# Wider idle matrix products, an earlier second row tile and reordered norms in the first stage of a hybrid decoder block

## The chip, the cores and the metric

The kernel runs on one core of one Trainium2 chip. The metric is the device time in microseconds (us) of one execution; lower is better. The engines are TensorE (PE, with its weight loads as PEld), VectorE (DVE), ScalarE (ACT), GpSimd (POOL) and SyncE (SP, which issues the loads). TensorE works on 128 x 128 weights, and its clock can be halved by a gate; the profile shows the granted share.

## The reference, cut to what matters

One decoder layer on `x` of 1024 rows by 1024 columns in fp32. A conditioning vector gives a scale and shift per column (`mod`), with which the normed rows become `h`; then `h` is multiplied by a wide weight matrix, and two mixers and projections follow.

```python
mod = jax.nn.silu(c) @ ada_w + ada_b
shift, scale, gate = jnp.split(mod, 3, axis=-1)
h = rms_norm(x, norm_w) * (1 + scale[:, None, :]) + shift[:, None, :]
proj = h @ w_in
...
return x + gate[:, None, :] * (merged @ w_out)
```

Only the way from `x` and `c` to `h`, and the first columns of `h @ w_in`, are touched by the change.

## The kernel before

The first stage makes `h` transposed: columns of `x` on the partitions, rows on the free axis. It works in eight turns n = 0 to 7; turn n handles one tile of 128 columns, k = KS[n] with KS = (0, 4, 1, 5, 2, 6, 3, 7), and each turn has two halves h of 512 rows. `xt[t]` (t = 0 to 7) are the tiles of 128 rows of `x`, each 128 x 1024. In the profile a tile is named without its number: `x` for all of `xt`.

What happens to a row tile, in order: ACT squares it and sums (`square`; for t = 1 DVE does it, `square_v`), DVE adds epsilon and POOL raises to the power -0.5 (`factors`, result `rs`), and DVE multiplies the tile in place, 512 columns at a time (`normed(t, half, V)`; half 0 serves k < 4, half 1 the rest). `transposes(n, h)` then has PE transpose four 128 x 128 blocks into the PSUM tile `px`, and `rows_of_h(n, h)` applies scale and shift: it writes the fp32 result `hf`, its fp32r rounding (`b11h`, `b`, `b21h` and the like) and the rest that rounding left (`b11l` and so on).

What happens to the conditioning: three small loads land in `pk`; PE transposes it into `pp`; DVE copies it to `par` and makes silu(c) (`sc`, `scz`) with ACT's tanh. `matvec(n)` multiplies `scz` by a tile `aw` of the conditioning weights on PE into `pm`, ACT copies this out as `row`, `modulation_product(n)` turns it to the partitions on PE, and `modulation(n)` makes scale and shift `md` on DVE.

`first_products(n)` is a generator: each step issues one product of 512 columns of `h` by the first 256 columns of the weights, in fp32r, into the PSUM tiles `acc`. The weights `w0r` are split into `w0h` (ACT) and `w0l` (DVE) by `split_w0`. Turns 0 and 1 are written out by hand; from turn 2 on, `prepare(n)` returns the work that is placed between certain steps of the products.

The order on every engine is the order in which the code is written (the calls are pinned); each engine takes its instructions in that order and waits at each for what it needs. Loads go through SP's queue, in written order too.

`warm(n)` issues idle products: they multiply constants into the PSUM tile `pd`, whose contents are overwritten before use. They stand at five places, with 11, 4, 3, 10 and 5 of them: ahead of the transpose of `pk`, ahead of `matvec(0)`, ahead of `modulation_product(0)`, ahead of `transposes(0, 0)` and ahead of `transposes(0, 1)`. None stands between the transposes and the first `acc` product.

Of the kernel before, what the change touches and what calls it, by code (L numbers as in the profile page):

```python
# [16 lines left out]
P = 128  # L17
# [3 lines left out]
NCH = S // P  # L21
# [14 lines left out]
def hybrid_kernel(  # L36
# [7 lines left out]
    V, A, G, PE = nc.vector, nc.scalar, nc.gpsimd, nc.tensor  # L44
# [26 lines left out]
    def cst(shape, name, dt=F32):  # L71
        return const.tile(shape, dt, name=name, tag=name)
# [6 lines left out]
    pin = tc.keep_in_program_order  # L79

    def mm(acc, l, r, first=True, last=True):
        pin(PE.matmul(acc, l, r, start=first, stop=last))  # L82

    def tp(dst, src, idn):
        pin(PE.transpose(dst, src, idn))  # L85

    def f32(t):
        return t.bitcast(F32)

    def load(dst, src):  # L90
        pin(nc.sync.dma_start(dst, src))
# [4 lines left out]
    ident = cst([P, P], "ident")  # L96
    make_identity(nc, ident)
    ones = cst([P, P], "ones")
# [51 lines left out]
    def ax(name, tag="pm"):  # L150
        return psum0.tile([P, 512], F32, name=name, tag=tag, bufs=2 if tag == "px" else 1)
# [17 lines left out]
    def wide(name, dt=F32):  # L169
        return w4[0].tile([P, S], dt, name=name, tag="w4", bufs=w4[1])  # L170


    with tc.tile_pool(name="p0", bufs=1, reuse_waits="tile") as p0:
        pxs = {(0, 0): ax("px0_0", "px")}
        pp = ax("pp")
        pd = ax("pd", "pd")
# [3 lines left out]
        aw, wk = {}, {}  # L180
# [7 lines left out]
        def hf_tile(k, h):  # L188
            if k not in hf2:
                hf2[k] = wide(f"hf{k}")  # L190
            return hf2[k][:, h * 512 : (h + 1) * 512]
# [30 lines left out]
        def split_w0(n):  # L222
            raw, hi, lo = wk[n]
            pin(A.copy(hi, raw))
            pin(V.tensor_sub(lo, raw, f32(hi)))
# [14 lines left out]
        def late_loads():  # L240
            load(wd, w_in[:, COL_DT : COL_DT + NH].rearrange("(k p) c -> p k c", p=P))

        def warm(n):

            for _ in range(n):
                mm(pd[:, 0:P], ident, ones)

        warm(11)
        tp(pp[:, 0:P], pk, ident)
        pin(V.tensor_copy(par, pp[:, 0:P]))  # L250
        pin(V.tensor_scalar_add(par[:, 24:32], par[:, 24:32], 1.0))
# [6 lines left out]
        def matvec(n):  # L258

            pms[n] = pm = ax(f"pm{n}")  # L260
            for i in range(KT):
                q = i % 4
                mm(pm[32 * q : 32 * q + 32, 0:256], scz[:, i, :], aw[n][:, i].rearrange("p j c -> p (j c)"),
                   i < 4, i >= 4)
            row = p0.tile([P, 256], F32, name=f"row{n}", tag="row", bufs=2)
            pin(A.copy(row, pm[:, 0:256]))
            mds[n] = row

        def modulation_product(n):

            pm, row = pms[n], mds[n]
            for j in range(2):
                mm(pm[:, 256 + j : 257 + j], row[:, j * P : (j + 1) * P], ones[:, 0:1])

        def modulation(n):

            k, pm = KS[n], pms[n]
            md = p0.tile([P, 2], F32, name=f"md{n}", tag="md", bufs=3)
            pin(V.tensor_add(md[:, 0:1], pm[:, 256:257], par[:, 16 + k : 17 + k]))
            pin(V.scalar_tensor_tensor(md[:, 1:2], pm[:, 257:258], par[:, 24 + k : 25 + k], par[:, 8 + k : 9 + k],  # L280
                                       op0=ALU.add, op1=ALU.mult))
            mds[n] = md

        def transposes(n, h):
            k = KS[n]
            px = pxs[n, h] if n + h == 0 else ax(f"px{n}_{h}", "px")
            for i in range(4):
                tp(px[:, i * P : (i + 1) * P], xt[4 * h + i][:, k * P : (k + 1) * P], ident)
            pxs[n, h] = px

        def rows_of_h(n, h, meanwhile=None):
            k, md, px = KS[n], mds[n], pxs[n, h]
            if k < 4 and h:
                b12 = wide(f"b12_{k}", F32R)
                hh, hl = b12[:, 0:512], b12[:, 512:1024]
            else:
                nm = ("b11" if k < 4 else ("b21", "b22")[h])
                hh, hl = bop[nm][0][k % 4], bop[nm][1][k % 4]
            if n + h:
                hfs[k, h] = hf_tile(k, h)  # L300
            hf = hfs[k, h]
            if n + h:
                for t in (hh, hf):
                    pin(A.activation(t, px, AF.Identity, scale=md[:, 1:2], bias=md[:, 0:1]))
            else:
                pin(V.tensor_scalar(hf, px, md[:, 1:2], md[:, 0:1], op0=ALU.mult, op1=ALU.add))
                pin(V.tensor_copy(hh, hf))
            if meanwhile:
                meanwhile()
            pin(V.tensor_sub(hl, hf, f32(hh)))  # L310
            hhs[n, h] = (hh, hl)
# [6 lines left out]
        def t_sum(k, i):  # L318

            b11, b12, b21, b22 = (hfs[k + 4 * (j // 2), j % 2] for j in range(4))  # L320
            a, b, c = ((b11, b12, b11), (b12, b22, b12), (b22, b22, b11), (b21, b21, b22))[i]
            pin(V.tensor_sub(a, b, c))

        def t_part(k, nm):

            t_split(nm, k, hfs[{"t1": (k, 0), "t3": (k, 1), "t2": (k + 4, 1), "t4": (k + 4, 0)}[nm]])
# [11 lines left out]
        def dt_products(k):  # L338

            for q, (kk, h) in enumerate(((k, 0), (k + 4, 0), (k, 1), (k + 4, 1))):  # L340
                mm(pd[32 * q : 32 * q + 32, :], wd[:, kk, :], hfs[kk, h], k == 0, k == 3)

        def halves(n):

            return (0, 1) if KS[n] < 4 or n == 1 else (1, 0)
# [5 lines left out]
        def square(t):  # L351
            pin(A.activation(junk, xt[t], AF.Square, accum_out=sq0[:, t : t + 1]))

        def factors(a, b):
            bs = slice(a, b)
            pin(V.tensor_scalar_add(sq0[:, bs], sq0[:, bs], D * EPS))
            pin(G.tensor_tensor(rs[:, bs], sq0[:, bs], nhalf[:, bs], op=ALU.pow))

        def normed(t, half, eng):
            part = xt[t][:, half * 512 : (half + 1) * 512]  # L360
            if eng is A:
                pin(A.mul(part, part, rs[:, t : t + 1]))
            else:
                pin(V.tensor_scalar_mul(part, part, rs[:, t : t + 1]))
# [4 lines left out]
            pin(V.scalar_tensor_tensor(junk2, xt[t], 1.0, xt[t], op0=ALU.mult, op1=ALU.mult,  # L369
                                       accum_out=sq0[:, t : t + 1]))  # L370

        warm(4)
        square(0)
        factors(0, 1)
        square_v(1)
        factors(1, 2)
        matvec(0)
        warm(3)
        modulation_product(0)
        normed(0, 0, V)  # L380
        modulation(0)
# [8 lines left out]
        pin(V.tensor_sub(wk[0][2], wk[0][0], f32(wk[0][1])))  # L390
        for t in range(4, NCH):
            square(t)
        warm(10)
        transposes(0, 0)
        rows_of_h(0, 0, lambda: (factors(4, 5), factors(5, 6)))
        load_aw(2)
        load_w0(2)
# [10 lines left out]
        normed(7, 0, V)  # L408
        for t in range(1, 4):
            normed(t, 1, V)  # L410
        warm(5)
        transposes(0, 1)
        rows_of_h(0, 1)
        transposes(1, 0)
        for t in (4, 5):
            normed(t, 1, V)
        matvec(1)
        split_w0(1)
        for _ in range(2):
            next(start)  # L420
        modulation_product(1)
        modulation(1)
        for t in (6, 7):
            normed(t, 1, V)
        rows_of_h(1, 0)
        for _ in start:
            pass

        def prepare(n):

            a, b = halves(n)
            k = (n - 2) // 2

            def second():
                modulation_product(n)
                transposes(n, b)
                if n % 2 == 0:
                    dt_products(k)
                modulation(n)
                if n % 2:  # L440
                    t_sum(k, 2)
                    t_sum(k, 3)
                rows_of_h(n, a)
                if n % 2 == 0:
                    t_sum(k, 0)
                rows_of_h(n, b)
                if n % 2:
                    t_part(k, "t3")
                    t_part(k, "t2")
                else:  # L450
                    t_sum(k, 1)

            if n == 2:
                return {
                    4: lambda: (transposes(1, 1), rows_of_h(1, 1), matvec(n)),
                    8: lambda: (transposes(n, a), second()),
                }
            return {2: lambda: (matvec(n), transposes(n, a)), 7: second}
# [12 lines left out]
        for n in range(1, KT):  # L471
            todo = prepare(n + 1) if n + 1 < KT else {}
            for at, _ in enumerate(first_products(n), 1):
                if at == 1 and n + 2 < KT:
                    load_aw(n + 2)
                    load_w0(n + 2)
                if at in todo:
                    todo[at]()
                if at == 2 and n < KT - 1:
                    split_w0(n + 1)  # L480
                between(n, at)
# [1067 lines left out]
    fill = proj_a()  # L1549
# [68 lines left out]
    def slot_tile(name, dt=F32):  # L1618
        tag = room.pop(0)
        t = hp.tile([P, 512], dt, name=name, tag=tag)  # L1620
        tags_of[name] = tag
        return t
# [218 lines left out]
    for u, (nm, k) in enumerate(units):  # L1841
# [28 lines left out]
        if k == KT - 1:  # L1870
            for j in range(4):
                with tc.high_priority():
                    if nm in ("p1", "p3", "p5"):
                        t = slot_tile(f"{nm}_{j}")
# [200 lines left out]
```

## Time and profile before

| what | value |
|---|---|
| median of 3 runs | 1360.52 us (1359.84 to 1361.66) |
| the profiled execution | 1360.42 us |
| its span (first to last instruction) | 1358.4 us |
| PE busy | 1345.4 us, 99% of the span |
| DVE, ACT, POOL busy | 1055.1, 800.6, 198.8 us |
| chain that ended last | PE 92%, DVE 3%, DMA 3% |

The span is shorter than the execution by 2.0 us, which lie around it. The rows of a timeline give start, length, engine, line of the code, operation, tiles (output, then inputs), shape and the number of records that were merged into the row; in brackets stands the idle time of the engine ahead of it and what ended it. Rows overlap a little, because a matrix product's end lies behind the start of the next one. The first stage ends near 65 us.

### The profile page before, as it was taken

Reading aid. Unit: us, or ns where it says so; the run is one execution under the profiler, and the core shown is the slowest. Engines: PE = TensorE matmul, PEld = TensorE weight load, DVE = VectorE, ACT = ScalarE, POOL = GpSimd, SP = SyncE. Lnnn points to the kernel's source line nnn. Section 1 sums busy time; section 2 is a strip of 40 time slices with the busy share of each in tenths; the row PEclk is TensorE's granted clock in tenths of the full one; section 3 lists DMA queues with packets and bytes.
Section 4 is the critical chain, followed back from the end, with each engine's and each line's share of the span. In section 5 each row is a group of like instructions: output and inputs, shape, how many; then the busy total and the mean of one; then the engine's idle time right before and its main releaser. Section 6 shows DMA issues by size and latency. Waiting matters only on the chain.

```text
span 1358.4 us, 20100 instructions
## 1 busy us (share of the span) xinstructions
PE 1345.4 (99%) x6897; PEld 1112.8 (82%) x6897; DVE 1055.1 (78%) x1732; ACT 800.6 (59%) x1446; POOL 198.8 (15%) x197
## 2 busy tenths in 40 slices
PE   8999999999999999999999999999999999999997
PEld 6688888888888888888888888888888888888886
DVE  5777786687777888688887788458888877959976
ACT  5854666666666665466576655486877743233543
POOL 2000000000000000000000000007798981000002
PEclk9999999999999999999999999999999999999999
DMA  9675434433345667778656866489889987878913
GB/s 301 178 247 155 127 110 124 124 118 116 108 125 155 194 196 229 238 227 246 199 194 188 248 203 185 157 290 315 302 297 318 297 260 277 323 265 316 380 43 124
DMA packets 249577, 288.64 MB, mean 212 GB/s; under 512 B 16860, under 2 KB 196484, under 8 KB 249476
## 3 DMA queue, kind: packets, MB, share of 16 engines
q1 hardware_dynamic: 174868, 203.80, 47.2%
q10 hardware_dynamic: 74544, 83.57, 18.0%
q8 instruction: 54, 0.88, 0.3%
q14 instruction: 47, 0.39, 0.1%
q0 software_dynamic: 64, 0.00, 0.0%
HBM read 199.82 MB, written 87.49 MB: 212 GB/s over the span
## 4 chain that ended last, share of the span: by engine, by line
PE 92%; DVE 3%; DMA 3%; issue 1%; ACT 0%; SPq 0%; POOL 0%; POOLq 0%; DVEq 0%; ACTq 0%
PE pma L82 7%; PE xcb L584 6%; PE xuz L584 6%; PE xz L584 6%; PE xx L584 6%; PE xg L584 6%; PE yuz L584 3%; PE yx L584 3%; PE ycb L584 3%; PE yz L584 3%; PE vx L989 3%; PE yg L584 3%; PE ox L1913 3%; PE yi L82 2%; PE sp L82 2%; PE oy L1913 2%
## 5 line engine op out<-in xcount | busy, mean ns | idle before, releaser
L1158 POOL TENSOR_SCALAR_AFFINE_SELECT dcy<-dcy 128x1024 f32<-128x1024 f32 x32 | 35.3, 1104 | 788.3 <-ACT ea L1154 785.9
L1166 ACT ACTIVATE dcy<-dcy,nacs 128x128 f32<-128x128 f32 x256 | 78.3, 389 | 2.6 <-POOL dcy L1158 2.0
L1182 DVE TENSOR_TENSOR dcy<-dcy,pc 128x1024 f32<-128x1024 f32 x32 | 39.0, 1219 | 8.0 <-PE pc L85 5.8
L1264 POOL TENSOR_TENSOR yz<-y,sl 128x512 f32<-128x512 f32 x32 | 44.7, 1397 | 2.5
L82 PE MATMUL pma<-yh,wah 128*128 128x512 f32 x128 | 43.2, 418 | 0.0
L82 PE MATMUL pma<-yh,wal 128*128 128x512 f32 x128 | 42.6, 413 | 0.0
L82 PE MATMUL pma<-yl,wah 128*128 128x512 f32 x128 | 40.2, 395 | 0.0
L1154 ACT ACTIVATE ea<-dcy 64x512 f32<-64x512 f32 x64 | 39.8, 622 | 0.4
L1059 ACT ACTIVATE ac<-ac 128x1024 f32<-128x1024 f32 x32 | 33.9, 1060 | 10.2 <-DVE ac L1057 10.1
L1189 ACT COPY bn<-pc 128x256 f32<-128x256 f32 x32 | 11.9, 372 | 47.0 <-DVE dcy L1182 46.8
L1263 POOL TENSOR_TENSOR y<-y,ym 128x512 f32<-128x512 f32 (+1 forms) x32 | 37.5, 1171 | 1.7 <-DVE ym L1261 1.7
L1057 DVE SCALAR_TENSOR_TENSOR ac<-c2x,cwt,ac 128x1023 f32<-128x1023 f32 (+2 forms) x24 | 30.7, 1279 | 8.6 <-ACT ac L1055 8.5
L1057 DVE SCALAR_TENSOR_TENSOR ac<-c2cb,cwt,ac 128x1023 f32<-128x1023 f32 (+2 forms) x24 | 30.7, 1279 | 8.1 <-ACT ac L1055 8.0
L1928 POOL TENSOR_TENSOR r<-r,fnw 128x512 f32<-128x512 f32 x4 | 6.1, 1528 | 205.7 <-ACT junk L1926 205.7
L82 PE MATMUL yi<-dcy,xd 128*64 128x128 f32 x512 | 35.0, 279 | 0.0
L1652 DVE SCALAR_TENSOR_TENSOR yn<-yn,par,rb 128x512 f32<-128x512 f32 x32 | 26.1, 823 | 10.8 <-DMA yn<-yb_d 10.8
L1261 DVE TENSOR_TENSOR ym<-yn,ea 128x512 f32<-128x512 f32 (+1 forms) x32 | 19.9, 622 | 18.5 <-PE yn L82 18.4
L82 PE MATMUL sp<-xe,bn 128*128 128x256 f32 x112 | 32.7, 409 | 0.0
L82 PEld LDWEIGHTS yn<-sl,st 128*128 128x128 f32 x224 | 29.7, 191 | 2.8 <-POOL st L1227 0.4
L82 PEld LDWEIGHTS yi<-dcy,xd 128*64 128x64 f32 x512 | 27.3, 136 | 5.7 <-issue 3.2
L1057 DVE SCALAR_TENSOR_TENSOR ac<-c1cb,cwt,ac 128x1023 f32<-128x1023 f32 (+2 forms) x24 | 30.7, 1278 | 1.3 <-ACT ac L1055 1.3
L1021 ACT ACTIVATE vm<-vm,vr 128x128 f32<-128x128 f32 x64 | 25.5, 482 | 9.7 <-DMA vm<-v_d 9.2
(2985 smaller groups left out, 4369.6 us busy)
## 6 DMA issues: line engine op xcount, KB each, us to landing
sl<-s_d SPq DMA_DIRECT2D x32, 768.0 KB
s_d<-ac ACTq DMA_DIRECT2D x32, 512.0 KB
wb_d<-wbb ACTq DMA_DIRECT2D x32, 512.0 KB
dcy<-acs_d SPq DMA_DIRECT2D x32, 512.0 KB
av<-in_w_in_dram SPq DMA_DIRECT2D x36, 256.0 KB
aw<-in_ada_w_dram SPq DMA_DIRECT2D x16, 512.0 KB
wbr<-in_w_proj_b_dram SPq DMA_DIRECT2D x32, 256.0 KB
yb_d<-yz ACTq DMA_DIRECT2D x32, 256.0 KB
```

The source lines that it names most:

```text
L82: pin(PE.matmul(acc, l, r, start=first, stop=last))
L584: pin(PE.matmul(ps, lw[:, k * P : (k + 1) * P], r[k], start=first and n + k == 0, stop=n == 2 and k == 3, skip_group_check=not first))
L989: pin(PE.matmul(ps[pn][j], l[:, j * P : (j + 1) * P], r, start=nm in ("p1", "p5", "p2") and n + units[i][1] == 0, stop=n == 2 and k == 3, ...
L1057: V.scalar_tensor_tensor(ac[:, s:], cc[:, : S - s], conv_wt[:, 3 - s, i : i + 1], ac[:, s:], op0=ALU.mult, op1=ALU.add)
L1059: A.activation(ac, ac, AF.Silu)
L1154: link("A", lambda: A.activation(ea[hh * HD : (hh + 1) * HD], dcy.rearrange("p (j e) i l -> p e j (i l)", e=2)[hh * HD : (hh + 1) * HD, hh ...
L1158: link("G", lambda: G.affine_select(out=d8, in_=d8, compare_op=ALU.is_ge, fill=-1e30, base=0, pattern=[[0, 2 * HPG], [1, P]], channel_mult ...
L1166: link("A", lambda: A.activation(dcy[:, h, i, :], dcy[:, h, i, :], AF.Exp, bias=sub[:, i, h : h + 1]))
L1182: link("V", lambda: V.tensor_tensor(d3, d3, pc[:, 0:256].unsqueeze(1).to_broadcast([P, HPG, 256]), op=ALU.mult))
L1263: link("G", lambda: G.tensor_add(y1[:, :, t0:], y1[:, :, t0:], m[:, :, t0:]))
L1264: link("G", lambda: G.tensor_mul(yz, y1, sl[:, 4:6]))
L1913: pin(PE.matmul(ps, a[:, tsl], b[:, cs], start=first and n + j == 0, stop=n == 2 and j == 3, skip_group_check=not first))
```

## The change

There are three parts. First, an idle product is now 512 columns wide where the count allows: the argument of `warm` counts units of 128 columns, four of them go into one product, and what is left is issued 128 wide. The moving operand is the second half of the tile `hf` of column tile 0, set to 1.0 by a memset on DVE, in place of `ones`. The counts become 24, 8, 5, 20 and 9, and 4 and 9 units are added inside `transposes(0, 0)`, behind its third and its fourth transpose. Second, the turn `(1, 1)` of the second column tile (rows 512 to 1023) has its transposes ahead of the products of turn 1 instead of at the fourth step of those products, and its `rows_of_h` at the second step instead of the fourth. Third, `normed(4..7, 1)` go ahead of `rows_of_h(0, 1)` in one run, where they stood in two pairs behind it; the two parts of `split_w0(1)` are written apart, with DVE's subtraction behind `modulation(1)`; and `transposes(1, 0)` precede `rows_of_h(0, 1)`.

```diff
+        idle = hf_tile(0, 1)
+        V.memset(idle, 1.0)
+
         def warm(n):
 
-            for _ in range(n):
-                mm(pd[:, 0:P], ident, ones)
-
-        warm(11)
+            for k in [512] * (n // 4) + [P] * (n % 4):
+                mm(pd[:, 0:k], ident, idle[:, 0:k])
+
+        warm(24)
         tp(pp[:, 0:P], pk, ident)
...
-        def transposes(n, h):
+        def transposes(n, h, fill=()):
...
                 tp(px[:, i * P : (i + 1) * P], xt[4 * h + i][:, k * P : (k + 1) * P], ident)
+                if fill:
+                    warm(fill[i])
...
-        warm(4)
+        warm(8)
         square(0)
...
         matvec(0)
-        warm(3)
+        warm(5)
         modulation_product(0)
...
-        warm(10)
-        transposes(0, 0)
+        warm(20)
+        transposes(0, 0, (0, 0, 4, 9))
...
-        warm(5)
+        warm(9)
         transposes(0, 1)
+        transposes(1, 0)
+        for t in range(4, NCH):
+            normed(t, 1, V)
         rows_of_h(0, 1)
-        transposes(1, 0)
-        for t in (4, 5):
-            normed(t, 1, V)
         matvec(1)
-        split_w0(1)
+        pin(A.copy(wk[1][1], wk[1][0]))
         for _ in range(2):
             next(start)
         modulation_product(1)
         modulation(1)
-        for t in (6, 7):
-            normed(t, 1, V)
+        pin(V.tensor_sub(wk[1][2], wk[1][0], f32(wk[1][1])))
         rows_of_h(1, 0)
         for _ in start:
             pass
+        transposes(1, 1)
...
             if n == 2:
                 return {
-                    4: lambda: (transposes(1, 1), rows_of_h(1, 1), matvec(n)),
+                    2: lambda: rows_of_h(1, 1),
+                    4: lambda: matvec(n),
                     8: lambda: (transposes(n, a), second()),
                 }
```

Three places show how the instructions stand now. A row has the line, the operation, the output and inputs by their numbered names, the shape and a count. On PE at the very start, before:

```order
L82 MATMUL pd_229<-ones_140,ident_135 128x128 x11
L85 MATMUL pp_228<-ident_135,pk_242 128x128
L82 MATMUL pd_229<-ones_140,ident_135 128x128 x4
L82 MATMUL pm0_304<-aw0_240,scz_244 32x256 x8
L82 MATMUL pd_229<-ones_140,ident_135 128x128 x3
L82 MATMUL pm0_304<-ones_140,row0_313 128x1 x2
L82 MATMUL pd_229<-ones_140,ident_135 128x128 x10
L85 MATMUL px0_0_227<-ident_135,x0_232 128x128
```

On PE at the same place, with the change (`hf0_241` is the tile whose second half is the idle operand):

```order
L82 MATMUL pd_229<-hf0_241,ident_135 128x512 x6
L85 MATMUL pp_228<-ident_135,pk_242 128x128
L82 MATMUL pd_229<-hf0_241,ident_135 128x512 x2
L82 MATMUL pm0_298<-aw0_240,scz_244 32x256 x8
L82 MATMUL pd_229<-hf0_241,ident_135 128x512
L82 MATMUL pd_229<-hf0_241,ident_135 128x128
L82 MATMUL pm0_298<-ones_140,row0_307 128x1 x2
L82 MATMUL pd_229<-hf0_241,ident_135 128x512 x5
L85 MATMUL px0_0_227<-ident_135,x0_232 128x128
```

The real work stands in the same order; between its steps are fewer but wider idle products. On DVE behind the norms of the first halves, before (`x4` to `x7` are the row tiles, `b12_0` the fp32r tile of turn 0's second half, `md1` the scale and shift of turn 1):

```order
L364 TENSOR_SCALAR x3_235<-x3_235,rs_291 128x512
L310 TENSOR_TENSOR b12_0_396<-hf0_241,b12_0_396 128x512
L364 TENSOR_SCALAR x4_236<-x4_236,rs_291 128x512
L364 TENSOR_SCALAR x5_237<-x5_237,rs_291 128x512
L225 TENSOR_TENSOR w0l1_268<-w0r1_266,w0h1_267 128x256
L279 TENSOR_TENSOR md1_424<-pm1_407,par_146 128x1
L280 SCALAR_TENSOR_TENSOR md1_424<-pm1_407,par_146 128x1
L364 TENSOR_SCALAR x6_238<-x6_238,rs_291 128x512
L364 TENSOR_SCALAR x7_239<-x7_239,rs_291 128x512
L310 TENSOR_TENSOR b21l0_206<-hf4_429,b21h0_202 128x512
```

On DVE at the same place, with the change:

```order
L369 TENSOR_SCALAR x3_235<-x3_235,rs_287 128x512
L369 TENSOR_SCALAR x4_236<-x4_236,rs_287 128x512
L369 TENSOR_SCALAR x5_237<-x5_237,rs_287 128x512
L369 TENSOR_SCALAR x6_238<-x6_238,rs_287 128x512
L369 TENSOR_SCALAR x7_239<-x7_239,rs_287 128x512
L315 TENSOR_TENSOR b12_0_395<-hf0_241,b12_0_395 128x512
L282 TENSOR_TENSOR md1_415<-pm1_399,par_146 128x1
L283 SCALAR_TENSOR_TENSOR md1_415<-pm1_399,par_146 128x1
L428 TENSOR_TENSOR w0l1_268<-w0r1_266,w0h1_267 128x256
L315 TENSOR_TENSOR b21l0_206<-hf4_419,b21h0_202 128x512
```

All four norms stand ahead of the subtraction and of `md1`, and the split of the weights stands behind `md1`. On PE around the second turn, before (`b21h0` is turn 1's first half, `px1_1` its second half transposed):

```order
L82 MATMUL acc1_231<-b12_0_396,w0h0_256 128x512
L82 MATMUL acc0_230<-b21h0_202,w0h1_267 128x512
L82 MATMUL acc1_231<-b21h0_202,w0h1_267 128x512
L82 MATMUL acc0_230<-b21h0_202,w0l1_268 128x512
L82 MATMUL acc1_231<-b21h0_202,w0l1_268 128x512
L85 MATMUL px1_1_450<-ident_135,x4_236 128x128
```

On PE at the same place, with the change:

```order
L85 MATMUL px1_1_427<-ident_135,x4_236 128x128
L85 MATMUL px1_1_427<-ident_135,x5_237 128x128
L85 MATMUL px1_1_427<-ident_135,x6_238 128x128
L85 MATMUL px1_1_427<-ident_135,x7_239 128x128
L82 MATMUL acc0_230<-b21h0_202,w0h1_267 128x512
```

The four transposes of turn (1, 1) moved ahead of the four products that wait for `b21h0`.

## The prediction

> **What bounds the kernel now.** I read the page first, then the PE rows of the timeline from 0 to 32 us, the PE waits after that, the granted clock in narrow stretches, and the DVE and ACT rows beside the first stage.
>
> ```profile
> span 1358.4 us, 20100 instructions
> PE 1345.4 (99%) x6897; PEld 1112.8 (82%) x6897; DVE 1055.1 (78%) x1732; ACT 800.6 (59%) x1446; POOL 198.8 (15%) x197
> ...
> PE 92%; DVE 3%; DMA 3%; issue 1%; ACT 0%; SPq 0%; POOL 0%; POOLq 0%; DVEq 0%; ACTq 0%
> ```
>
> PE is busy for 99% of the span and makes up 92% of the chain that ended last. What is left to win or lose in the first stage is what the start of the stage's real work is moved by. The PE rows (start, length, records; in fp32 a product leaves two records, a transpose one):
>
> ```profile
> 1.53 4.65 PE L82 MATMUL pd<-ones,ident 128*128 128x128 f32 x22 [1.53 <-POOL ident masks.py:199]
> 7.20 0.30 PE L85 MATMUL pp<-ident,pk 128*128 128x128 f32 x1 [1.02 <-DMA pk<-in_ada_b_dram]
> 7.34 1.06 PE L82 MATMUL pd<-ones,ident 128*128 128x128 f32 x8
> 8.74 1.07 PE L82 MATMUL pm<-aw,scz 128*32 128x256 f32 x16 [0.34 <-DVE scz L255]
> 9.74 0.94 PE L82 MATMUL pd<-ones,ident 128*128 128x128 f32 x6
> 10.51 0.50 PE L82 MATMUL pm<-ones,row 128*128 128x1 f32 x4
> 10.88 2.48 PE L82 MATMUL pd<-ones,ident 128*128 128x128 f32 x20
> 13.19 0.72 PE L85 MATMUL px<-ident,x 128*128 128x128 f32 x3
> 14.50 0.33 PE L85 MATMUL px<-ident,x 128*128 128x128 f32 x1 [0.59 <-DVE x L364]
> 16.29 1.19 PE L82 MATMUL acc<-b11h,w0h 128*128 128x512 f32 x2 [1.46 <-DVE sq L356]
> ...
> 18.99 1.41 PE L82 MATMUL pd<-ones,ident 128*128 128x128 f32 x10
> 20.24 1.33 PE L85 MATMUL px<-ident,x 128*128 128x128 f32 x8
> 21.50 1.07 PE L82 MATMUL pm<-aw,scz 128*32 128x256 f32 x16
> 22.50 0.73 PE L82 MATMUL acc<-b,w0h 128*128 128x512 f32 x2
> ...
> 24.07 0.63 PE L82 MATMUL acc<-b,w0h 128*128 128x512 f32 x2
> 25.24 0.72 PE L82 MATMUL acc<-b21h,w0h 128*128 128x512 f32 x2 [0.53 <-ACT b21h L304]
> ...
> 26.27 0.60 PE L85 MATMUL px<-ident,x 128*128 128x128 f32 x4
> 26.79 1.07 PE L82 MATMUL pm<-aw,scz 128*32 128x256 f32 x16
> ```
>
> PE's waits here are 1.53, 1.02, 0.34, 0.59, 1.46 and 0.53 us, 5.5 in all. Idle products stand ahead of the 1.02, the 0.34 and, with three transposes between, the 0.59; none ahead of the 1.46 and the 0.53. After 25 us, the waits of PE are these two, of which only the second lies behind matvec(2) at 26.79:
>
> ```profile
> PE acc L82 <- ACT b21h L304: 0.5, 1, 0.5
> PE oy L1913 <- DVE wlt L1802: 0.4, 1, 0.4
> ```
>
> So a shift of matvec(2) goes to the end of the program almost whole; at most 0.4 us of it can be taken up later. I therefore follow PE up to matvec(2) and compare with 26.79. The granted clock (columns: PE busy, records, clock, DMA):
>
> ```profile
> 15.75:16.00 0.25, 0.00 (x0) 0.70 0.98 393
> 16.00:16.25 0.25, 0.00 (x0) 0.50 1.11 442
> ...
> 19.00:19.25 0.25, 0.25 (x3) 0.50 1.16 283
> 19.25:19.50 0.25, 0.25 (x4) 0.98 1.19 291
> ```
>
> The clock is halved from 15.85 (0.70 over a quarter microsecond) to 19.26: 3.41 us, after a stretch in which PE waited 0.59 and 1.46. Six acc products from 16.29 to 18.99 pay for it. The first eleven idle products also ran at half speed for the most part: 4.65/11 = 0.42 us each, against 2.48/10 = 0.25 for the ten at 10.88. If the gate steps on a grid of 3.41 us, it opened at 19.26 - 4 x 3.41 = 5.6 in this execution; an estimate. The Trainium skill ("TensorE: Matmul & The Clock Gate", What's actually happening) says that the window is 3413 ns and free-running, so another execution has another phase; the trace agrees on the length, and one profile can't show the phase of others. The same page (Why this matters for your kernels) wants gaps under about 3 us to keep the clock up; here a longest gap of 1.46 in a thinly used window was enough to lose it, so the measurement decides, and for the change, which fills that window.
>
> **What one wide idle product costs.** Before has no 512-wide fp32 product over all 128 columns. Nearest are the 256-wide ones and, as the floor, the 512-wide fp32r ones, which leave one record each:
>
> ```profile
> 910.19 0.59 PE L82 MATMUL sp<-xe,bn 128*128 128x256 f32 x2
> 910.41 0.59 PE L82 MATMUL sp<-xe,bn 128*128 128x256 f32 x2
> ```
> ```profile
> 65.06 10.88 PE vx L989 x48
> ```
>
> Consecutive 256-wide fp32 records start 0.22 apart, so such a product takes 0.44. The 128-wide ones at 10.88 take (13.19 - 10.88)/10 = 0.23. Time goes with columns: 512 wide is 0.87, and 1.74 at half clock. The floor is two records at the fp32r pace, 2 x 10.88/48 = 0.45; the ceiling four 128-wide ones, 0.92. I take 0.87, since the 256-wide row is the same kind of instruction.
>
> **The change, part by part.** Idle work was 33 units of 128 columns (11+4+3+10+5). It becomes 79 (24+8+5+20+4+9+9), in 19 products of 512 and 3 of 128: 19 x 0.87 + 3 x 0.23 = 17.2 us at full clock, against 33 x 0.23 = 7.6. The waits to be filled are 5.5. So the filling is larger than the holes by about 4 us, and the question is where it lands. The rows of the other engines:
>
> ```profile
> 1.10 0.27 DVE L199 MEMSET scz<- 128x256 f32 x1
> ...
> 13.96 0.48 DVE L364 TENSOR_SCALAR x<-x,rs 128x512 f32<-128x512 f32 x1 [0.44 <-POOL rs L357]
> ...
> 14.87 0.81 DVE L306 TENSOR_SCALAR hf<-px,md 128x512 f32<-128x512 f32 x1
> ...
> 19.51 1.67 DVE L364 TENSOR_SCALAR x<-x,rs 128x512 f32<-128x512 f32 x4 [0.44 <-POOL rs L357]
> 22.36 0.69 DVE L310 TENSOR_TENSOR b<-hf,b 128x512 fp32r<-128x512 f32 x1 [1.18 <-ACT hf L304]
> ...
> 24.16 0.21 DVE L280 SCALAR_TENSOR_TENSOR md<-pm,par 128x1 f32<-128x1 f32 x1
> ```
> ```profile
> 9.88 0.37 ACT L266 COPY row<-pm 128x256 f32<-128x256 f32 x1 [0.76 <-PE pm L82]
> ...
> 17.32 1.06 ACT L352 ACTIVATE junk<-x 128x1024 f32<-128x1024 f32 x1 [0.18 <-DMA x<-in_x_dram]
> 24.41 0.78 ACT L304 ACTIVATE b21h<-px,md 128x512 fp32r<-128x512 f32 x1 [1.09 <-DVE md L280]
> ```
>
> - The memset of the idle operand is twice scz's 0.27 behind 1.37: PE starts at 1.9 instead of 1.53.
> - warm(24), six wide products: to 5.6 at half clock (5.6 - 1.9)/1.74 = 2.1 of them, then 3.9 x 0.87, so they end at 8.97. pk has landed by 7.20, but its transpose stands behind them: +1.77.
> - 0.14 for pp, then two wide products (before four narrow): 10.85. scz is ready 1.54 behind pp's start, at 10.51, so this fill also overlaps the end by 0.3. matvec(0) takes 1.00: 11.85. The row copy ends some 0.5 later, at 12.4.
> - One wide, one narrow: 12.95. Modulation product 0.37: 13.32.
> - warm(20), five wide: 17.67. On DVE, x3's factor has its place behind par and the squares; these move by no more than matvec(0)'s 2.1 to 2.4, so x3 is normed by 16.9 and PE is the later of the two.
> - Three transposes at 0.13 ((26.79 - 26.27)/4): 18.06; one wide product: 18.93; x3's transpose, 0.33 long: 19.26. Before it ended at 14.83: **+4.43**, all of it PE's own queue.
> - hf, b11h follow on DVE: 14.83 to 16.29 is 1.46, so acc could start at 20.72; warm(9) behind the transposes takes 1.97 and ends at 21.03. The six acc products then run at full clock, 6 x 0.227 = 1.36 instead of 18.99 - 16.29 = 2.70: 22.39. The clock's dip is gone and 1.34 us come back.
> - warm(9): 24.36. The eight transposes take 1.26, but need x's second halves: the run of four on DVE at 19.51 moves by 4.43 to 23.94 and ends at 25.61 (ACT's last square, 17.32, moves by the row copy's 2.1 and ends at 20.6, in time). Last transpose done, matvec(1) at 25.74, before 21.50: **+4.24**.
> - From 21.50 to the end of the last acc pair's issue (24.07 + 0.46) are 3.03: 28.77. transposes(1, 1), now here, 0.52: 29.29. They are no longer behind b21h, so 0.52 leaves there, where PE had waited 0.53.
> - Is b21h in time? DVE now does x4 to x7's four second halves before the b subtraction: 25.61 + 1.67 = 27.28, + 0.69 and the two md steps, 28.3; ACT's b21h 0.78 to 29.1. Before 29.29: in time, by 0.2. Postponed w0l and w0h casts stand behind md and cost nothing as long as this margin holds; without it PE waits out the difference.
> - Four acc products, 26.27 - 25.24 = 1.03: matvec(2) at 30.32 against 26.79: **+3.53**. aw's third tile is needed that much later than before; no new DMA is issued, and the queue's order is the same. matvec(1)'s buffer comes free 4.2 later, 9 us ahead of its reuse at matvec(3).
>
> The profiled execution took 1360.42 us, 0.1 below the median of the runs. 1360.42 + 3.53 = 1363.95; the forecast is **1364.0**, 0.26% slower.
>
> **Rivals.**
>
> *The wide product costs half as much (not slower).* Place: every idle product. If a 512-wide one ran at the floor, 0.45, the fills would last about as long as before (six wide in 2.7 at full clock against 2.5 for eleven narrow, five wide in 2.25 against 2.3) and warm(20) would again end at 13.13. Then the dip goes, the eight transposes are held by x7's norm as before, and the moved transposes fill PE's 0.53: I get matvec(2) at about 25.8, -1.0, 1359.4. Going through the same steps at 0.60 gives -0.4 and at 0.70 gives +1.0, so it decides at a price of about 0.64. Against it are the 256-wide rows (0.44 already). The Trainium skill ("TensorE: Matmul & The Clock Gate", Back-to-back issue gap) gives N/2.4 + 2.5 ns, 0.216 at 512 columns; with two records that is 0.43, an estimate, and this rival. By that rule a 256-wide record would take 0.11; the trace has 0.22, so it does not hold for fp32 here. Chance 0.10.
>
> *The gate opens late.* PE's fill starts at 1.9. On the 3.41 grid a full window ends by 8.7 at the latest; warm(24) then ends (8.7 - 5.6)/2 = 1.55 later: +5.1, 1365.5. For it: the phase is not set by the program. Chance of an opening after 7.0: 0.12.
>
> *The gate opens early.* The window up to 2.19 had 0.66 of PE work and did not open it; the earliest opening is then 2.6, and the fill ends 1.5 earlier: +2.0, 1362.4. Chance of an opening before 4.5: 0.12.
>
> *The delay is taken up later.* Only 0.38 us of PE waits stand behind 26.79; gaps too short for the view might hold a little more. 1362 to 1363, chance 0.06.
>
> **How the numbers follow.** The likeliest case, the gate between 4.5 and 7.0, has 0.60 and gives 1363.4 to 1364.7. About 0.2% (2.7 us, 1363.2) is what a measurement of this kernel can tell from no change. Slower by more: all of the likeliest but its lower edge, the late gate, little of the others: 0.68. Within: most of the early gate, the half price and the later uptake, and the lower edge: 0.28. Faster by more than 0.2% would need more than the half-priced case gives: 0.04. The range leaves out the half price and thin tails, and adds the runs' own spread of about 1 us at each side: 1361.6 to 1366.4.
>
> **What the profile after would show.** Right: idle products with starts of one product 0.87 apart at full clock, six of them ending near 9; pp's transpose started late with no DMA wait; no PE wait worth naming from 1.9 to 25; clock never halved after its opening; x3's transpose near 19, matvec(2) near 30.3. Wrong, if the wide products are 0.45 to 0.6 long, if pp still starts at 7.2, if b21h is waited for by much (the DVE order then costs more than I count), or if matvec(2)'s shift and the shift of the end differ by over half a microsecond.

## The result

The changed kernel takes 1365.7 us (median of 7 runs, 1364.52 to 1366.01) against 1360.54 for the kernel before in the same comparison: 1.0033 times as long, 95% interval 1.0022 to 1.0044. Slower, as forecast, and by more: 5.2 us where 3.5 were forecast. The profiled execution took 1364.52 us, the fastest of the seven; that matters below.

The page of the changed kernel:

```profile
span 1362.4 us, 20059 instructions
PE 1352.6 (99%) x6875; PEld 1110.7 (82%) x6875; DVE 1056.6 (78%) x1733; ACT 800.7 (59%) x1446; POOL 199.4 (15%) x197
...
PE 93%; POOL 3%; issue 1%; DVE 1%; DMA 0%; SPq 0%; ACT 0%; POOLq 0%; DVEq 0%; ACTq 0%
```

PE is "busier" by 7.2 us, and the span is 4.0 longer. PE's rows of the first stage, up to matvec(2):

```profile
2.06 7.20 PE L82 MATMUL pd<-hf,ident 128*128 128x512 f32 x12 [2.06 <-DVE hf L244]
9.10 0.27 PE L85 MATMUL pp<-ident,pk 128*128 128x128 f32 x1
9.21 1.88 PE L82 MATMUL pd<-hf,ident 128*128 128x512 f32 x4
11.02 1.07 PE L82 MATMUL pm<-aw,scz 128*32 128x256 f32 x16
12.02 1.35 PE L82 MATMUL pd<-hf,ident 128*128 128x512 f32 x4
13.20 0.50 PE L82 MATMUL pm<-ones,row 128*128 128x1 f32 x4
13.57 4.54 PE L82 MATMUL pd<-hf,ident 128*128 128x512 f32 x10
17.95 0.49 PE L85 MATMUL px<-ident,x 128*128 128x128 f32 x3
18.27 1.02 PE L82 MATMUL pd<-hf,ident 128*128 128x512 f32 x2
19.13 0.27 PE L85 MATMUL px<-ident,x 128*128 128x128 f32 x1
19.24 2.10 PE L82 MATMUL pd<-hf,ident 128*128 128x512 f32 x6
21.10 0.70 PE L82 MATMUL acc<-b11h,w0h 128*128 128x512 f32 x2
...
22.57 2.10 PE L82 MATMUL pd<-hf,ident 128*128 128x512 f32 x6
24.50 1.51 PE L85 MATMUL px<-ident,x 128*128 128x128 f32 x8
25.95 1.07 PE L82 MATMUL pm<-aw,scz 128*32 128x256 f32 x16
...
29.38 0.73 PE L82 MATMUL acc<-b21h,w0h 128*128 128x512 f32 x2
...
30.49 1.07 PE L82 MATMUL pm<-aw,scz 128*32 128x256 f32 x16
```

After the first idle product nothing in these rows has an idle time in brackets. The waits of the whole program on PE are two:

```profile
PE pd L82 <- DVE hf L244: 2.1, 1, 2.1
PE oy L1919 <- DVE wlt L1808: 0.3, 1, 0.3
```

So the change did what it says: the waits are filled, and PE is late. Five wide products take 17.95 - 13.57 = 4.38, 0.876 each, and nothing that they make is used. Who waits now is DVE (its rows at x's norms and at the first `hf`):

```profile
15.22 1.04 DVE L369 TENSOR_SCALAR x<-x,rs 128x512 f32<-128x512 f32 x2 [0.27 <-POOL rs L362]
...
19.45 0.81 DVE L311 TENSOR_SCALAR hf<-px,md 128x512 f32<-128x512 f32 x1 [2.85 <-PE px L85]
```

The last norm that the first transposes need is done at 16.3, and PE comes to that tile at 19.13; DVE stands still for 2.85 us. matvec(2) starts 3.70 us later than before (30.49 against 26.79).

### The profile page after: what moved, and what is told of

The parts are those of the page before. It is cut to its first block, busy times and chain, and to the rows that moved or that the text cites. A ratio compares the mean times of both kernels' runs of the same rounds, so it can differ in the third digit from the quotient of the medians.

```text
span 1362.4 us, 20059 instructions
## 1 busy us (share of the span) xinstructions
PE 1352.6 (99%) x6875; PEld 1110.7 (82%) x6875; DVE 1056.6 (78%) x1733; ACT 800.7 (59%) x1446; POOL 199.4 (15%) x197
## 4 chain that ended last, share of the span: by engine, by line
PE 93%; POOL 3%; issue 1%; DVE 1%; DMA 0%; SPq 0%; ACT 0%; POOLq 0%; DVEq 0%; ACTq 0%
PE xcb L590 6%; PE xz L590 6%; PE xuz L590 6%; PE xx L590 6%; PE xg L590 6%; PE pma L82 5%; PE yuz L590 3%; PE yx L590 3%; PE ycb L590 3%; PE yp L1727 3%; PE yz L590 3%; PE vx L995 3%; PE yg L590 3%; PE ox L1919 3%; PE oy L1919 2%; PE yi L82 2%
## 5 line engine op out<-in xcount | busy, mean ns | idle before, releaser
L865 ACT CAST wbb<-wbr 128x512 fp32r<-128x512 f32 x32 | 19.8, 618 | 20.6 <-DMA wb_d<-wbb 18.9
```

## The experiments

All ratios are against the kernel before, run on the same chip in the same comparison. A difference in us is between the medians of one comparison.

**The order alone (e1_order).** The new order, the old idle products:

```diff
-        warm(24)
+        warm(11)
...
-            for k in [512] * (n // 4) + [P] * (n % 4):
-                mm(pd[:, 0:k], ident, idle[:, 0:k])
+            for _ in range(n):
+                mm(pd[:, 0:P], ident, ones)
...
```

> The new order of norms and transposes with the old idle products (11, 4, 3, 10, 5 of 128 columns, none inside the transposes). Theory A (the filling alone makes the change slow, the order is a small gain): the transposes of turn (1, 1) go into PE's 0.53 us wait, matvec(2) starts 0.5 to 0.9 us earlier than in the kernel before (near 26.1), 1359.6 to 1360.1 us. Rival B (the four norms ahead of the scale and shift cost part of the loss): matvec(2) no earlier than 26.8, 1360.5 us or more, and PE waits for b21h by over half a microsecond.

Measured: 1359.74 us against 1360.63, ratio 0.9994 (0.9985 to 1.0002). Rows of its PE timeline:

```profile
16.59 0.70 PE L82 MATMUL acc<-b11h,w0h 128*128 128x512 f32 x2 [1.46 <-DVE sq L358]
...
24.84 0.60 PE L85 MATMUL px<-ident,x 128*128 128x128 f32 x4
25.22 0.73 PE L82 MATMUL acc<-b21h,w0h 128*128 128x512 f32 x2
...
26.33 1.07 PE L82 MATMUL pm<-aw,scz 128*32 128x256 f32 x16
```

The transposes of turn (1, 1) sit where PE had waited 0.53 for b21h; matvec(2) is 0.46 earlier in this profile, just short of the 0.5 to 0.9 that were expected, and nearly all of that stays to the end. The gain is too small for the interval to tell from nothing. The interval's upper end is a loss of 0.3 us, and the profile shows neither of rival B's signs, a matvec(2) no earlier than 26.8 and a long wait for `b21h`: the order is no part of a loss of 5.2 us.

**The fills alone (e2_fill).** The old order with the new idle products. The edit puts the order of the kernel before back at all its places; the last of them:

```diff
...
-            2: lambda: rows_of_h(1, 1),
-            4: lambda: matvec(n),
+            4: lambda: (transposes(1, 1), rows_of_h(1, 1), matvec(n)),
```

> The new idle products with the old order. Theory A: all of the loss is here, and what the order wins is missing: matvec(2) near 31.2 (4.4 later than before) if the clock gate opens near 5.7, later by half of what the gate opens later; 1365.3 to 1367 us. Rival B: less than the changed kernel's loss, 1363.5 to 1364.5 us.

Measured: 1365.47 us against 1360.63 (5 runs), ratio 1.0037 (1.0024 to 1.0049): 4.8 us, the whole loss as far as the intervals can tell. Its profiled execution took 1366.53, and PE's rows say why it is so late:

```profile
2.06 8.44 PE L82 MATMUL pd<-hf,ident 128*128 128x512 f32 x12 [2.06 <-DVE hf L244]
10.34 0.27 PE L85 MATMUL pp<-ident,pk 128*128 128x128 f32 x1
...
30.75 0.73 PE L82 MATMUL acc<-b21h,w0h 128*128 128x512 f32 x2 [0.36 <-ACT b21h L309]
...
32.31 1.07 PE L82 MATMUL pm<-aw,scz 128*32 128x256 f32 x16
```

The same six products, begun at the same 2.06, take 8.28 up to pk's transpose instead of 7.04. At full clock they would take 6 x 0.876 = 5.26, and each microsecond at half clock adds a half: (7.04 - 5.26)/0.5 = 3.6 in the changed kernel's profile, 6.0 here. So the gate opened near 5.6 there and near 8.1 here. matvec(2) stands at 32.31; the expected 31.2, with half of the 2.4 us between 5.7 and 8.1 added, is 32.4. With the old order `b21h` is waited for again, 0.36 us.

**The right amount (e3_units).** The changed kernel, with the units cut to what the waits hold:

```diff
-        warm(24)
+        warm(12)
...
-        warm(8)
+        warm(4)
...
-        warm(5)
+        warm(3)
...
-        warm(20)
-        transposes(0, 0, (0, 0, 4, 9))
+        warm(10)
+        transposes(0, 0, (0, 0, 2, 5))
...
-        warm(9)
+        warm(5)
```

> The changed kernel with the idle work cut to what the waits hold: 12, 4, 3, 10, (0, 0, 2, 5) and 5 units, still issued 512 wide where they fit. Theory A (the amount of columns on PE's queue is what costs, not the width and not the order): pk's transpose at 7.2 again, x3's transpose near 14.5, no halved clock at the first acc products, matvec(2) near 25.9; 1359.3 to 1360.0 us. Rival C (wide products or the idle memset hurt by themselves): slower than the kernel before by 1 us or more.

Measured: 1360.3 us against 1360.63, ratio 0.9998 (0.9989 to 1.0007). Rival C is out: the interval ends below its 1 us, so wide products and the memset cost little or nothing where there is room. The first stage came out nearly as expected (matvec(2) at 26.15 instead of 25.9), the end did not. PE's rows:

```profile
7.23 0.30 PE L85 MATMUL pp<-ident,pk 128*128 128x128 f32 x1 [0.76 <-DMA pk<-in_ada_b_dram]
...
16.41 0.70 PE L82 MATMUL acc<-b11h,w0h 128*128 128x512 f32 x2 [0.38 <-DVE sq L361]
...
20.15 1.51 PE L85 MATMUL px<-ident,x 128*128 128x128 f32 x5 [0.60 <-DVE x L369]
...
26.15 1.07 PE L82 MATMUL pm<-aw,scz 128*32 128x256 f32 x16
...
1036.25 0.71 PE L82 MATMUL yn<-sl,st 128*128 128x128 f32 x4 [0.20 <-DVE st L1241]
```

matvec(2) is 0.64 earlier than before, and the products keep some 0.6 of that up to 1018 us. At 1019.6 PE waits 0.18 for POOL and the lead is 0.34; by 1039 the kernel is 0.34 late, and near 1288 it is level with the kernel before. Around 1036 us PE waits for a state (the tile `st`) that DVE and POOL make. Part of a gain can be lost there; what sets how much was not tried.

**The first fill alone (e4_first).** The kernel before with one edit:

```diff
-        warm(11)
+        idle = hf_tile(0, 1)
+        V.memset(idle, 1.0)
+        for _ in range(6):
+            mm(pd, ident, idle)
```

> The kernel before with one edit: the eleven idle products ahead of pk's transpose are six of 512 columns. Theory A with the gate's phase: pk's transpose near 9.1 if the gate opens near 5.7, and later by half of any later opening, up to 10.6; of the 1.9 us and more, DVE's and ACT's chain to x3's norm passes on some 1.2, so 1361.7 to 1363.5 us, with a spread over the runs of over 1 us. Rival D (the start is hidden behind the loads of x, and only the fills behind it cost): within 0.5 us of the kernel before.

Measured: 1361.88 us against 1360.63, ratio 1.0011 (1.0002 to 1.002). The runs go from 1361.38 to 1362.85, less far than those of the kernel before in the same comparison (1359.57 to 1362.14), so their spread says nothing of the gate. PE's rows:

```profile
2.06 7.52 PE L82 MATMUL pd<-hf,ident 128*128 128x512 f32 x12 [2.06 <-DVE hf L244]
9.42 0.27 PE L85 MATMUL pp<-ident,pk 128*128 128x128 f32 x1
...
18.12 0.70 PE L82 MATMUL acc<-b11h,w0h 128*128 128x512 f32 x2 [1.46 <-DVE sq L360]
...
28.12 1.07 PE L82 MATMUL pm<-aw,scz 128*32 128x256 f32 x16
```

pk's transpose is 2.2 late; matvec(2) 1.33. Here 7.36 us for the six, so the gate opened near 6.3. Rival D does not fit this profile: the start is not hidden behind the loads. The times alone would leave it room, since the interval goes from 0.3 to 2.7 us.

**Twelve units ahead of pk (f1_first12).** The changed kernel with `warm(12)` for `warm(24)`.

> The changed kernel with 12 units (three wide products) ahead of pk's transpose instead of 24; the other fills stay. Theory A (every wide product beyond a wait delays PE by its own length, and the first fill's length depends on when the clock gate opens): pk's transpose at 7.2 whenever the gate opens, 1.9 us earlier than in the changed kernel's profile, matvec(2) near 28.6, and the median falls by more than 1.9, by 2.5 to 3.5 us (1362.2 to 1363.2), since the later openings cost nothing any more. Rival E (the gate's phase is not what lifts the median over the profiled run): the median falls by 1.9 or less, 1363.8 us or more.

Measured: 1363.01 us against 1360.92, ratio 1.0017 (1.0008 to 1.0026). Its excess is 2.1 us where the changed kernel's is 5.2: 3.1 less, for 1.8 us of PE time less in the profiles of both:

```profile
2.06 5.46 PE L82 MATMUL pd<-hf,ident 128*128 128x512 f32 x6 [2.06 <-DVE hf L244]
7.32 0.35 PE L85 MATMUL pp<-ident,pk 128*128 128x128 f32 x1
```

Three products took 5.26, all at half clock, and still ended when pk had just landed. An opening up to 7.3 costs nothing here; in the changed kernel it does. The median lies where theory A put it, but rival E is not excluded: each of the two ratios is uncertain by over 1 us to each side, so that a difference of 3.1 is not clear of 1.9. And the runs of this kernel go from 1361.67 to 1364.05, further apart than those of the changed kernel, though by theory A the gate's part is gone here.

**Half the middle fill (f2_mid10), and more of it (f3_mid28).** `warm(10)` and `warm(28)` for `warm(20)` in the changed kernel.

> The changed kernel with warm(10) instead of warm(20) ahead of the first transposes. Theory A: two wide and two narrow products instead of five wide ones, 2.2 us off PE's queue; x's norms are done by 16.3, so x3's transpose comes 2.2 earlier and the median falls by 1.9 to 2.3 us (1363.4 to 1363.8). Rival F (DVE's norms hold x3 anyway, so that fill is hidden): less than 0.7 us.

> The changed kernel with warm(28) instead of warm(20): two more wide products at the same place. Theory A: 2 x 0.87 = 1.75 us later at matvec(2) and at the end, 1367.2 to 1367.7 us. Rival F: no more than 0.5 us later.

Measured: f2_mid10 1362.93 us against 1360.92, ratio 1.0014 (1.0005 to 1.0023); f3_mid28 1366.61 (4 runs), ratio 1.0045 (1.0031 to 1.0058). The first moved by more than expected, the second by less. The fill, the first transpose behind it and matvec(2) in the profiles, f2_mid10 and then f3_mid28:

```profile
2.06 8.42 PE L82 MATMUL pd<-hf,ident 128*128 128x512 f32 x12 [2.06 <-DVE hf L244]
...
14.79 2.41 PE L82 MATMUL pd<-hf,ident 128*128 128x512 f32 x8
17.03 0.49 PE L85 MATMUL px<-ident,x 128*128 128x128 f32 x3
...
29.58 1.07 PE L82 MATMUL pm<-aw,scz 128*32 128x256 f32 x16
```
```profile
2.06 8.46 PE L82 MATMUL pd<-hf,ident 128*128 128x512 f32 x12 [2.06 <-DVE hf L244]
...
14.83 6.25 PE L82 MATMUL pd<-hf,ident 128*128 128x512 f32 x14
20.93 0.49 PE L85 MATMUL px<-ident,x 128*128 128x128 f32 x3
...
33.47 1.07 PE L82 MATMUL pm<-aw,scz 128*32 128x256 f32 x16
```

The fill lasts 2.24 and 6.10 where it was 4.38: 2.14 less and 1.72 more, what the columns ask for. In both the gate opened near 8.1, which makes the start some 1.25 us later than in the changed kernel's profile. With that taken off, matvec(2) moves by 2.79 - 3.70 - 1.25 = -2.2 and 6.68 - 3.70 - 1.25 = +1.7: one for one, and rival F (DVE hides that fill) is out. At the end, f3_mid28 has given 0.6 back at the products that stand near 1288 us in the kernel before: PE no longer waits for `wlt` (a part of the last projection's weights that DVE makes). The changed kernel's profile has lost another 0.3 at those that stand near 1039 there. So only 0.8 of the 1.7 shows between the two profiled executions, with the start's 1.25 taken off, and 0.5 in the medians. These two account for the miss of f3_mid28 in the profiles. Why f2_mid10's median moved by 3.1 us, where its profile, the 1.25 taken off, moved by 2.3, stays open.

**The old narrow products in the right amount (f4_narrow).** e1_order with two and six narrow products inside the first transposes:

```diff
-        transposes(0, 0)
+        transposes(0, 0, (0, 0, 2, 6))
```

> The new order with the old narrow products (11, 4, 3, 10, 5), and 2 and 6 narrow ones inside the transposes, behind the third and the fourth. It differs from the right-sized kernel with wide products only in how the idle work is cut. Theory A: no halved clock at the first acc products, matvec(2) 0.4 to 0.9 us earlier than in the kernel before; 1359.6 to 1360.3 us, beside the kernel with the new order alone, and the first stage's gain can be lost again in the later stage near 1036 us, where the right-sized kernel's profile lost 0.98. Rival C (narrow products keep the clock up less than wide ones): halved clock at the acc products again.

Measured: 1359.39 us against 1360.92, ratio 0.9991 (0.9982 to 1.0000): the lowest ratio here, at the edge of what the interval can tell. The granted clock from 16.6 to 19.2 us (length, PE busy with records, clock, DMA share, GB/s), in the kernel before, e1_order, f4_narrow and e4_first:

```profile
16.60:19.20 2.60, 2.60 (x8) 0.50 1.19 300
```
```profile
16.60:19.20 2.60, 2.60 (x10) 0.68 1.18 301
```
```profile
16.60:19.20 2.60, 2.60 (x17) 1.00 1.18 302
```
```profile
16.60:19.20 2.60, 1.14 (x6) 1.00 1.18 301
```

With the fill inside the transposes, wide (e3_units, 1.00) or narrow, the clock does not fall, and rival C's halved clock is not seen. Without it the clock falls in the kernel before and in e1_order. But e4_first has no such fill either, waits 0.46 and then 1.46 us at the same place, and keeps its clock. So these waits do not always cost the clock, and one profile each does not show that the fill is what keeps it. Nor does it matter much here: f4_narrow's matvec(2) is no earlier than e1_order's (26.36, 26.33), because the next transposes then wait 0.60 for x7's norm instead:

```profile
20.37 1.52 PE L85 MATMUL px<-ident,x 128*128 128x128 f32 x5 [0.60 <-DVE x L366]
...
26.36 1.07 PE L82 MATMUL pm<-aw,scz 128*32 128x256 f32 x16
```

In these two profiles keeping the clock up is worth nothing by matvec(2).

## Why the prediction was right, and where it was off

The steps, against the changed kernel's profile: pk's transpose 8.97 forecast, 9.10 measured; matvec(0) 10.85, 11.02; first transposes 17.67, 17.95; x3's transpose done 19.26, 19.40; first acc product 21.03, 21.10; the eight transposes 24.36, 24.50; matvec(1) 25.74, 25.95; b21h's products 29.29, 29.38; matvec(2) 30.32, 30.49. Nearly all of the 0.17 is the start of PE, 2.06 instead of 1.9. That the steps agree so closely is in part luck: in this one execution the gate opened near 5.6, the value that had been taken over from the kernel before. In e2_fill, f2_mid10 and f3_mid28 it opened near 8.1, and pk's transpose stood some 1.25 us later.

- The price of a wide product, the main term: 0.87 from the 256-wide rows, 0.876 measured. The half-price rival is out with it.
- "All of it PE's own queue": shown by f2_mid10 and f3_mid28, one for one at matvec(2).
- The clock's dip gone: the acc products took 1.47 us (21.10 to 22.57) where they had taken 2.70 (16.29 to 18.99). The dip was taken as a fixed part of the kernel before, brought on by its waits. e4_first, with waits of 0.46 and 1.46, had none in its profile, so the 1.34 that come back belong to one execution.
- b21h in time by 0.2: its products follow the transposes with no wait; in e2_fill, with the old order, they wait 0.36. But the margin was only 0.05 us: ACT ended `b21h` at 29.33 and not at 29.1, since DVE's `md` waited 0.41 for PE's modulation product, a wait that the forecast left out, and the products start at 29.38.

```profile
28.55 0.78 ACT L309 ACTIVATE b21h<-px,md 128x512 fp32r<-128x512 f32 x1 [0.78 <-DVE md L283]
```

- "At most 0.4 us can be taken up later": short of the mark both ways. 0.6 was taken up in f3_mid28 at the products near 1288 us, and 0.3 was added in the changed kernel's profile at those near 1039 (times of the kernel before).
- What was mis-sized: the opening of the gate. I put the likeliest case between 4.5 and 7.0, around the 5.6 of one profile, and gave later openings 0.12. The profiles of kernels that start with six wide products opened near 5.6, 6.3, 8.1, 8.1 and 8.1. The profiled execution of the changed kernel, at 5.6, was the fastest of seven; an opening near 8.1 adds (8.1 - 5.6)/2 = 1.25 to its 1364.52, 1365.8, and five of the seven runs lie between 1365.68 and 1366.01. f1_first12, whose first fill an opening up to 7.3 can't lengthen, moves the same way: 3.1 us less for 1.8 us of work. The "late gate" rival had the right price; by these five profiles it should have had about half the chance. So 1365.7 lies above the likeliest case's 1363.4 to 1364.7, and the range holds it because it left room for the late gate. The openings of the unprofiled runs are not seen: that they make up the 1.1 us between the profile's excess of 4.1 and the median's 5.2 is inferred, and the spread of f1_first12's runs, 2.4 us, shows that something else varies as well.

The Trainium skill ("TensorE: Matmul & The Clock Gate", What's actually happening) says that the warm-up is a time and not a number of products, on a free-running window. By that rule twice the idle columns at the start can't open the gate sooner. The trace agrees: with 24 units or 12 the fill began at the same 2.06, and the openings, near 5.6 to 8.1 with 24 units, near 5.3 (e3_units, where the records' starts then go from 0.85 to 0.43 apart) and near 7.4 (f1_first12, whose three products ran at half pace throughout) with 12, went with the execution and not with the amount. About 3.4 us, which the same section gives for that time, did not hold: it was 3.2 to 6.1 us here.

## What to carry to other kernels

Idle products are there to keep the clock up, but they stand in the same queue as the work: size each fill to the wait that it fills, from the measured length of one product of that very type and width, and let the first fill end before the data behind it lands even at half clock. Doubling a fill is not a safe side to err on: every surplus microsecond of the middle fill went one for one into the next real products, and DVE waited 2.85 us for PE with the data ready. Where a term depends on a phase that the program doesn't set (here, where the gate's steps fall against the start), one profile is one draw; the range should come from the grid, not from the value seen.

## What the runs showed of the hardware

- An fp32 product with 128 columns of weights costs by the columns that it moves, in two records: 0.23 us at 128, 0.44 at 256, 0.876 at 512, where an fp32r one of 512 takes 0.227. Wide idle products are hardly cheaper per column than narrow ones (1.71 ns against 1.80). With 32 columns of weights, matvec's products of 256 took 1.00 us for eight, 0.125 each; why was not tried.
- In both profiles in which the clock fell it was halved for 3.41 us: 15.85 to 19.26 in the kernel before, 17.54 to 20.95 in e1_order. Four such steps back from 20.95 is 7.3, and e1_order's gate did open between 6.6, where its first fill ended at half pace, and 7.4, where the next products ran at full pace: the grid that the prediction assumed fits there too.
- The gate opened between 3.5 and 6.1 us after the first idle product in the five profiles that start with six wide ones, though PE worked without a break from 2.06. The clock column reads 1.00 in that time too (2.00 to 5.00 us in the changed kernel: below); the pace of the products, twice 0.876 us each in f1_first12, tells the half clock, the column does not.

```profile
2.00:5.00 3.00, 2.94 (x4) 1.00 1.03 274
```
